# Softmax weights of six heads turned by VectorE's 32x32 blocks and placed by a trip through DRAM, where identity matmuls turned them

## The chip, the cores and the metric

The kernel runs on one core of a Trainium2 chip. The metric is device time of the whole program in microseconds (us): before the change the median of three runs is 1448.64 us (1448.3 to 1448.99). A profiled execution is read beside it. In the text TensorE is PE in the profile (PEld are its weight loads), VectorE is DVE, ScalarE is ACT, GpSimd is POOL, and SyncE is SP, which here only issues DMAs (SPq).

## The reference

A decoder trunk of two layers over 512 tokens of width 1024, in float32. Layer 0 mixes tokens by dilated sliding-window attention in three groups of eight heads, layer 1 by a gated recurrence; each layer ends in a gated feed-forward part with a short convolution, and RMS norms stand before and after every part. Only the attention matters here:

```python
WINDOWS = (128, 512, 2048); DILATIONS = (1, 4, 16); HEADS_PER_GROUP = 8; HEAD_DIM = 128
logits = einsum('bxhnqd,bxhnkd->bxhnqk', qs, kk) * scale + bias        # masked: causal band
mx = max(logits); p = exp(logits - mx); s = sum(p)
o = einsum('bxhnqk,bxhnkd->bxhnqd', p, vv) / s;  lse = mx + log(s)
...
alpha = softmax(stack(lses), axis=0)                                   # over the three groups
o = sum(alpha[..., None] * stack(outs), axis=0) @ w_o
```

For one of the eight output heads, group 0 attends within the last 128 tokens ("local"). Groups 1 and 2 attend to tokens of the same residue modulo 4 and 16 ("strided"). The kernel takes both strided groups over the four residues r of the token number modulo 4: for each r there are 128 queries and 128 keys, and the mask for residue modulo 16 lies in the bias.

## The kernel before

Nearly all time goes to matrix products of weights with activations. Each float32 operand is split into a high part `whi`, copied by ACT (line 246), and a remainder `wlo`, subtracted by DVE (line 255), and three TensorE passes make one product (`mm3`, line 423; `product`, line 611). Weight blocks of one megabyte come in on SP's queue (`raw`, line 329); some are added up from two sources by accumulating DMAs that POOL issues (`sum`, line 301). A load is issued once an earlier block has been split, so SP mostly waits for DVE's remainders.

The program is written in the order in which every engine takes its instructions; nothing reorders it. Beside the stream of products run "sides": Python generators that are advanced at each tick, that is, after each tile of 24 products. `yield n` lets n ticks pass. A strided head (`strided`, line 1289) is such a side. Per head it goes through these steps, for the two groups gi = 0, 1:

- scores: per residue one matmul q.k into PSUM (line 1310, tile S), then DVE adds the bias table `toe` and takes the row maximum (line 1314, recorded at its helper, line 1231), leaving L, 128 queries by 4 residues x 128 keys;
- ACT takes the exponential of each residue's columns with its sum (line 1299);
- DVE multiplies both L by the reciprocal of the common denominator (line 1346), and prepares the factor c0 of the local head;
- TensorE transposes each residue's 128x128 block against the identity (line 1359, tile PT), since the next product needs keys on partitions; ACT copies the result from PSUM (line 1361). A small matmul (line 1364, tile c) turns c0 the same way;
- TensorE multiplies with the values vp (line 1378, tile O), adds the local head's output ow, turned by line 1382, and the head's output oT is kept for the projection.

Heads 0 to 5 run like this in pairs, heads 6 and 7 with `ahead` set: they start earlier and use a running maximum for the first group. Tiles of 128x512 come from one pool of 29 buffers (`gen`), PSUM from 8 banks. The values are written to DRAM (line 1168) and read back by residue (line 1218), and the local heads' outputs likewise (lines 1286 and 1294), all on SP.

DMAs of SP report on eight semaphores in turn, and the program makes an issue wait until the DMA eight places ahead on the same semaphore has landed.

## Time and profile before

| | us |
|---|---|
| median of three runs | 1448.64 |
| profiled execution, span | 1446.8 |
| TensorE busy in it | 1433.7 |
| DVE busy | 1021.0 |
| ACT busy | 682.9 |
| strided heads, from the first S to the last O | about 266 to 490 |

The profiled execution's span goes from its first to its last instruction. Rows of a timeline read: start, duration, engine, line, operation, out<-in by the names of the tiles without their numbers, shapes, count, and in brackets the idle time of the engine before it and what ended it. Several equal instructions that follow each other stand in one row. Rows of groups read: count, busy time, mean duration in ns, idle time before. A float32 matmul is recorded as two rows, a transpose against the identity as one.

### The profile page before, as it was taken

To read this page: it belongs to the slowest core of one execution; us is meant where nothing else is said; L and a number is where in the kernel's file an instruction comes from. 1 tells how busy PE (TensorE), PEld (TensorE's weight loads), DVE (VectorE), ACT (ScalarE), POOL (GpSimd) and SP (SyncE) were. 2 spreads that over 40 slices of the span, in tenths; PEclk is the share of its full clock that TensorE was granted. 3 is DMA by queue.
4 is the path that set the end of the run, shared out by engine and by line. 5 is a ranking of instruction groups with operands and counts; after the bars stand their busy time and mean duration, and the time that the engine had idled before them with its cause. 6 is when DMAs were issued, how large, how long until landed. Compare 5 with 4: busy or idle time off the path is not lost.

```text
span 1446.8 us, 18794 instructions
## 1 busy us (share of the span) xinstructions
PE 1433.7 (99%) x7261; PEld 1219.0 (84%) x7261; DVE 1021.0 (71%) x1786; ACT 682.9 (47%) x1145; POOL 103.9 (7%) x116
## 2 busy tenths in 40 slices
PE   8999999999999999999999999999999999999997
PEld 6888888888888898998888888988898998888886
DVE  7864353455554688887977678877879887977675
ACT  5443332344345454455545444469654455535441
POOL 1210010111000001000000020000001000000020
PEclk9999999999999999999999999999999999999999
DMA  8974645766526153655767683233144565677561
GB/s 257 255 209 134 156 123 159 207 150 198 189 81 219 59 162 110 160 156 131 197 185 172 184 249 129 89 117 106 69 133 118 157 169 122 190 189 175 175 189 58
DMA packets 163660, 227.43 MB, mean 157 GB/s; under 512 B 6280, under 2 KB 119440, under 8 KB 163570
## 3 DMA queue, kind: packets, MB, share of 16 engines
q1 hardware_dynamic: 132544, 175.36, 36.0%
q0 software_dynamic: 31024, 50.86, 19.3%
q8 instruction: 57, 0.93, 0.3%
q14 instruction: 33, 0.27, 0.1%
q10 hardware_dynamic: 2, 0.00, 0.0%
HBM read 209.39 MB, written 21.53 MB: 160 GB/s over the span
## 4 chain that ended last, share of the span: by engine, by line
PE 97%; DVE 2%; ACT 1%; DMA 0%; issue 0%; SPq 0%; DVEq 0%
PE ps L423 55%; PE vq L611 18%; PE acc L423 11%; PE vq L423 6%; PE gate L423 2%; PE tr L472 1%; PE S L1310 1%; PE S L1243 1%; PE O L1282 1%; PE O L1378 1%; DMA raw<-in_attn_w_qkv_dram 0%; PE PT L1265 0%; PE v L1138 0%; PE PT L1359 0%; DVE wlo L178 0%; DVE wlo L255 0%
## 5 line engine op out<-in xcount | busy, mean ns | idle before, releaser
L423 PE MATMUL ps<-hT,whi 128*128 128x512 f32 (+1 forms) x2528 | 726.1, 372 | 0.6 <-DVE hT L477 0.3
L423 PEld LDWEIGHTS ps<-hT,whi 128*128 128x128 f32 x2528 | 457.6, 189 | 81.8 <-ACT whi L246 1.3
L423 PE MATMUL ps<-hT,wlo 128*128 128x512 f32 (+1 forms) x1264 | 468.3, 370 | 0.0
L255 DVE TENSOR_TENSOR wlo<-raw,whi 128x1024 fp32r<-128x1024 f32 x233 | 280.1, 1217 | 11.4 <-ACT whi L246 10.7
L423 PEld LDWEIGHTS ps<-hT,wlo 128*128 128x128 f32 x1264 | 238.1, 188 | 40.9
L246 ACT ACTIVATE whi<-raw 128x1024 fp32r<-128x1024 f32 x233 | 239.9, 1051 | 48.6 <-DMA raw<-in_ffn_w_up_dram 17.7
L796 DVE SCALAR_TENSOR_TENSOR u<-ps,cols,u 128x511 f32<-128x511 f32 (+1 forms) x160 | 119.6, 748 | 92.7 <-ACT u L792 89.9
L611 PE MATMUL vq<-whi,A 128*128 128x512 f32 x448 | 142.5, 389 | 0.0
L246 ACT ACTIVATE whi<-sum 128x1024 fp32r<-128x1024 f32 x68 | 71.4, 1053 | 113.6 <-DMA sum<-in_attn_w_qkv_dram 70.6
L255 DVE TENSOR_TENSOR wlo<-sum,whi 128x1024 fp32r<-128x1024 f32 x68 | 82.1, 1219 | 29.0 <-ACT whi L246 29.0
L423 PE MATMUL acc<-whi,ahi 128*128 128x512 f32 x256 | 100.9, 394 | 0.0
L423 PE MATMUL acc<-whi,alo 128*128 128x512 f32 x256 | 99.8, 390 | 0.0
L423 PE MATMUL acc<-wlo,ahi 128*128 128x512 f32 x256 | 99.6, 389 | 0.0
L611 PEld LDWEIGHTS vq<-whi,A 128*128 128x128 f32 x448 | 84.1, 188 | 17.6
L792 ACT ACTIVATE u<-ps,cols 128x512 f32<-128x512 f32 x80 | 61.6, 770 | 74.4 <-PE ps L423 74.4
L611 PE MATMUL vq<-wlo,A 128*128 128x512 f32 x224 | 87.1, 389 | 0.0
L806 ACT ACTIVATE u<-u 128x512 f32<-128x512 f32 x48 | 30.4, 633 | 99.7 <-DVE u L796 99.7
L611 PE MATMUL vq<-whi,T 128*128 128x512 f32 x192 | 62.2, 395 | 0.0
L423 PEld LDWEIGHTS acc<-whi,alo 128*128 128x128 f32 x256 | 48.1, 188 | 10.2
L423 PEld LDWEIGHTS acc<-wlo,ahi 128*128 128x128 f32 x256 | 48.1, 188 | 9.6
L423 PEld LDWEIGHTS acc<-whi,ahi 128*128 128x128 f32 x256 | 48.1, 188 | 9.6
L1120 DVE COPY qk<-ps 128x512 f32<-128x512 f32 x24 | 16.5, 688 | 51.2 <-PE ps L423 51.1
(250 smaller groups left out, 1814.9 us busy)
## 6 DMA issues: line engine op xcount, KB each, us to landing
raw<-in_ffn_w_up_dram SPq DMA_DIRECT2D x44, 1024.0 KB
raw<-in_attn_w_qkv_dram SPq DMA_DIRECT2D x25, 1024.0 KB
raw<-in_ffn_w_down_dram SPq DMA_DIRECT2D x16, 1024.0 KB
sum<-in_ffn_w_down_dram POOLq DMA_DIRECT2D x16, 1024.0 KB, 8.9
raw<-in_attn_w_qkv_dram SPq DMA_DIRECT2D x16, 512.0 KB
sum<-in_attn_w_qkv_dram POOLq DMA_DIRECT2D x16, 512.0 KB, 8.1
sum<-in_ffn_w_down_dram SPq DMA_DIRECT2D x8, 1024.0 KB
raw<-in_lru_w_in_dram SPq DMA_DIRECT2D x8, 1024.0 KB
```

The lines of the kernel that those rows point to most:

```text
L246: nc.scalar.activation(hi, raw, AF.Copy)
L255: nc.vector.tensor_tensor(lo, raw, hi.bitcast(F32), op=ALU.subtract)
L423: mm(dst, l[a], r[b], start=start and n == 0, stop=stop and n == 2)
L472: nc.tensor.transpose(ps[:, k * P : (k + 1) * P], xs[i][:, k * P : (k + 1) * P], ident)
L611: mm(banks[u], act(a)[:, 2 * j + k, u * P : (u + 1) * P], W[b][:, k, :], start=(j, k, n) == (0, 0, 0), stop=(j, k, n) == (1, 1, 2),)
L792: nc.scalar.activation(u, ps, AF.Identity, scale=cc[:, j : j + 1], bias=cc[:, 48 + j : 49 + j])
L796: nc.vector.scalar_tensor_tensor(u[:, d:], ps[:, : S - d], wc, u[:, d:], op0=ALU.mult, op1=ALU.add)
L806: nc.scalar.activation(u, u, AF.Gelu_apprx_tanh)
L1120: nc.vector.tensor_copy(dst, src)
L1243: mm(Sp[a // 2][:, o + lo : o + 256], q[hh][:, a * P : (a + 1) * P], k[hh][:, k0 : (a + 1) * P], start=True, stop=True)
L1282: mm(po[:, a * P : (a + 1) * P], pts[a, j], vtile(v, a - 1 + j, h % 4), start=j == js[0], stop=j == 1)
L1310: mm(ps[:, c], q[hh][:, c], k[hh][:, c], start=True, stop=True)
```

## The change

For heads 0 to 5 (not `ahead`), the turn of the weights is made without TensorE:

- L is laid out differently: `strips` puts residue r's keys 32 j to 32 j + 31 at columns 128 j + 32 r, so that scores, exponentials and the multiplication go through four runs of 32 columns per residue.
- Right after each multiplication DVE transposes L in blocks of 32x32 into a new tile LT: each block is turned in its place, but blocks are not exchanged across partitions.
- One tick later LT is written to a DRAM tile `std` (256 KB, one DMA on SP), and two ticks after that it is read back into PT by four DMAs of 64 KB on SP, which put each block where it belongs: 32 partitions, four runs of 128 elements each.
- The four transposes per group on TensorE, their PSUM bank and ACT's copy are gone. Heads 6 and 7 stay as they were. The ticks between multiplication and O are as many as before (1 + 2 + 4 against 3 + 4).

```diff
+        def strips(t):
+            return t.rearrange("p (j m k) -> p j m k", j=4, m=4)
...
+        def to_dram(t, ms, name):
+            d = dp.tile([P, 512], F32, name=name)
+            nc.sync.dma_start(strips(d)[:, :, ms, :], strips(t)[:, :, ms, :])
+            return d
+
+        def from_dram(d, ms):
+
+            t = gen(s="PT")
+            t4 = strips(t)
+            for j in range(4):
+                src = d.rearrange("(i k) (j m q) -> j k i m q", k=32, j=4, m=4)[j]
+                nc.sync.dma_start(t4[32 * j : 32 * j + 32, :, ms, :], src[:, :, ms, :])
+            return t.rearrange("p (i m q) -> p m i q", i=4, m=4)
...
+            def of_residue(L, r):
+                if ahead:
+                    return L[:, r * P : (r + 1) * P]
+                return strips(L)[:, :, r, :]
...
-                        L[:, c], L[:, c], AF.Exp, bias=neg[:, r : r + 1],
+                        of_residue(L, r), of_residue(L, r), AF.Exp, bias=neg[:, r : r + 1],
...
+                    if ahead:
+                        scores(L[:, c], ps[:, c], T[:, :P], at)
+                    else:
+                        scores(of_residue(L, r), in_strips(ps[:, c]), in_strips(T[:, :P]), at)
...
+                else:
+                    L4 = strips(L)
+                    by = of.unsqueeze(1).unsqueeze(3).to_broadcast([P, 4, 4, 32])
+                    nc.vector.tensor_tensor(L4, L4, by, op=ALU.mult)
+                    LT = gen(s="LT")
+                    nc.vector.transpose(LT, L)
+                    turned.append(LT)
...
-            yield 2 if ahead else 3
-            pts = []
-            for L in Ls:
-                ps = psum("PT")
...
+            else:
+                yield 1
+                placed = [to_dram(t, all_, f"std{h}{gi}") for gi, t in enumerate(turned)]
+                yield 2
+                pts = [from_dram(d, all_) for d in placed]
...
-                    mm(po[:, c], vtile(v, r, 2 * gi + hh), pts[gi][:, c], start=gi == 0, stop=gi == 1)
+                    mm(po[:, c], vtile(v, r, 2 * gi + hh), pts[gi][:, r], start=gi == 0, stop=gi == 1)
```

In the order of instructions this moves three places. On PE, where head 0's weights were turned, between the last product of a tile ps and the next product vq; first before the change, then now:

```order
L423 MATMUL ps_2531<-hT_86,whi_2319 128x512
L423 MATMUL ps_2531<-hT_85,wlo_2320 128x512
L1359 MATMUL PT_2558<-ident,L_2284 128x128 x4
L1359 MATMUL PT_2565<-ident,L_2296 128x128 x4
L1364 MATMUL c_2572<-s_2357,back 128x16
L611 MATMUL vq_2589<-whi_2405,T_417 128x512
```

```order
L423 MATMUL ps_2547<-hT_86,whi_2319 128x512
L423 MATMUL ps_2547<-hT_85,wlo_2320 128x512
L1407 MATMUL c_2584<-s_2361,back 128x16
L611 MATMUL vq_2601<-whi_2409,T_417 128x512
L611 MATMUL vq_2601<-wlo_2410,T_417 128x512
```

The eight transposes are gone and nothing else on PE has moved; the line of the small matmul is 1407 in the new file. On DVE, at the multiplication of head 1 (L474 and L477 are its two tiles of weights, wlo484 and wlo498 the remainders of the next two blocks of sum), now:

```order
L625 TENSOR_TENSOR v493_2474<-c489_2420,vq491_2448 128x512
...
L1368 RECIPROCAL s481_2394<-s480_2393 128x4
L1380 TENSOR_TENSOR L474_2374<-L474_2374,s481_2394 128x512
L1382 STREAM_TRANSPOSE LT494_2488<-L474_2374 128x512
L1380 TENSOR_TENSOR L477_2386<-L477_2386,s481_2394 128x512
L1382 STREAM_TRANSPOSE LT495_2491<-L477_2386 128x512
L1384 TENSOR_TENSOR s482_2395<-s482_2395,s481_2394 128x4
L1386 TENSOR_TENSOR s496_2494<-s482_2395,res_129 128x16
L255 TENSOR_TENSOR wlo484_2410<-sum54_230,whi483_2409 128x1024
L255 TENSOR_TENSOR wlo498_2497<-sum54_230,whi497_2496 128x1024
```

The two STREAM_TRANSPOSE rows are new, the rest stood there in the same order; they are now ahead of the remainders. On SP, from the write of values to the second load after it, before the change and now, with the semaphores that each waits for (DMAHW0 to DMAHW7 are the eight of SP's DMAs in turn):

```order
L329 DMA raw483_2409<-in_attn_w_qkv_dram 128x8x256 [waits DVE_49]
L1168 DMA vrows2_2411<-v490_2469 128x512 [waits DMAHW3_49,DVE_49]
L1168 DMA vrows2_2411<-v491_2470 128x512 [waits DMAHW4_49,DVE_49]
L329 DMA raw503_2529<-in_attn_w_qkv_dram 128x8x256 [waits DMAHW5_49,DVE_49]
L329 DMA raw532_2648<-in_attn_w_qkv_dram 128x4x256 [waits DMAHW6_49,DMAHW2_49,DVE_49]
L329 DMA raw532_2648<-in_attn_w_qkv_dram 128x4x256 [waits DMAHW7_49]
```

```order
L1168 DMA vrows2_2415<-v493_2474 128x512 [waits DMAHW4_49,DVE_49]
L1243 DMA std00_2479<-LT466_2355 128x512 [waits DMAHW5_49]
...
L1243 DMA std11_2535<-LT495_2491 128x512 [waits DMAHW0_49,DVE_49]
L329 DMA raw507_2545<-in_attn_w_qkv_dram 128x8x256 [waits DMAHW1_49,DVE_49]
L1252 DMA PT510_2574<-std00_2479 32x4x128 [waits DMAHW5_49,DMAHW2_49,PE_49]
L1252 DMA PT510_2574<-std00_2479 32x4x128 [waits DMAHW3_49]
...
L1252 DMA PT511_2579<-std01_2481 32x4x128 [waits DMAHW1_49]
L1252 DMA PT523_2631<-std10_2533 32x4x128 [waits DMAHW2_49,PE_49]
...
L1252 DMA PT524_2636<-std11_2535 32x4x128 [waits DMAHW1_49]
L329 DMA raw532_2656<-in_attn_w_qkv_dram 128x4x256 [waits DMAHW2_49,DVE_49]
```

The four writes stand ahead of a megabyte load and the sixteen reads of heads 0 and 1 (PT510, PT511, PT523, PT524) behind it; the next load comes after all of them. For heads 2 and 3 a load and four writes of values stand between the two groups of eight reads; for heads 4 and 5 the sixteen again follow a load, with one load of ow after the first eight.

## The prediction

> **What bounds the kernel now.** I read the head of the page first, then the chain that ended last, the waits of TensorE, and the stretch in which the strided heads run.

> ```profile
> span 1446.8 us, 18794 instructions
> PE 1433.7 (99%) x7261; PEld 1219.0 (84%) x7261; DVE 1021.0 (71%) x1786; ACT 682.9 (47%) x1145; POOL 103.9 (7%) x116
> ...
> PE 97%; DVE 2%; ACT 1%; DMA 0%; issue 0%; SPq 0%; DVEq 0%
> ...
> PE tr L472 <- DVE xs L512: 2.5, 1, 2.5
> ...
> 262.00:490.00 228.00, 227.76 (x1188) 194.19 (x1187) 121.27 (x344) 94.36 (x223) 19.18 (x24) 1.00 0.56 166
> ```

> The fourth line is the chain by engine, the fifth the longest wait that TensorE has, the last a row of the view by windows, with busy time of PE, PEld, DVE, ACT and POOL, the granted clock, the DMA share and GB/s. TensorE is busy 227.76 of 228 us in the strided heads and 97% of the chain is its own work. So a matmul row taken out there shortens the run by its own length, as long as everything that TensorE needs still comes in time, while work put on DVE (121 us of 228), ACT (94) or the queues is paid only where it makes TensorE wait. That is the whole question.

> **What is removed.** The view of the tile PT from 262 to 450 us holds the six changed heads, and the timeline of PE shows one of them:

> ```profile
> L1359 PE MATMUL PT<-ident,L x48: 270/272/273, 297.5 to 446.2; 128*128 128x128 f32 x48
> L1361 ACT ACTIVATE PT<-PT x12: 583/594/610, 308.2 to 446.7; 128x512 f32<-128x512 f32 x12
> ...
> 297.24 0.39 PE L423 MATMUL ps<-hT,wlo 128*128 128x512 f32 x1
> 297.47 1.03 PE L1359 MATMUL PT<-ident,L 128*128 128x128 f32 x8
> 298.34 0.29 PE L1364 MATMUL c<-s,back 128*128 128x16 f32 x2
> ...
> 298.80 0.40 PE L611 MATMUL vq<-wlo,T 128*128 128x512 f32 x1
> ```

> The 270 ns of one row overlap with the next, so the price is taken from starts: eight transposes from 297.47 to 298.34, 0.87 us, 0.109 each. Nothing in that list is idle before them. Six heads give 6 x 0.87 = 5.2 us. The small matmul c behind them stays. On ACT 12 x 0.594 = 7.1 us of evictions go; ACT is not on the path, so I count nothing for it.

> [...]

> **What DVE gets.** Twelve block transposes of 128x512, which no row of this kernel has. Nearest rows, of DVE from 262 to 490 us (count, busy us, mean ns):

> ```profile
> L255 DVE TENSOR_TENSOR wlo<-raw,whi 128x1024 fp32r<-128x1024 f32 x34 | 40.7, 1217 | 1.8 <-ACT whi L246 1.8
> L1346 DVE TENSOR_TENSOR L<-L,s 128x512 f32<-128x512 f32 x16 | 10.3, 688 | 0.3
> ```

> Below: nothing under half of 688 ns, since the same 512 columns are read and written; above: 1217 ns, as if it read twice as much. I take 0.69, the row of the same size: 8.3 us in all, on an engine with over 100 us to spare here. The scores, exponentials and products go through 4 x 32 instead of 128 columns in a row. They move as many elements; I take no extra, and as the upper end twice the duration.

> On average DVE has room; one stretch has not. The timeline of DVE, ACT's row of the first exponential there, and DVE's row in the windows:

> ```profile
> 283.23 0.29 DVE L1231 CUSTOM_DVE_ANT_0 L<-S,toe 128x128 f32<-128x128 f32 x1 [7.65 <-DMA toe<-skew]
> 285.82 0.39 ACT L1299 ACTIVATE L<-L,s 128x128 f32<-128x128 f32 x1
> 290.46 1.28 DVE L625 TENSOR_TENSOR v<-c,vq 128x512 f32<-128x512 f32 x2 [3.66 <-ACT c L1179]
> 292.47 1.29 DVE L1346 TENSOR_TENSOR L<-L,s 128x512 f32<-128x512 f32 x2
> 293.96 2.35 DVE L255 TENSOR_TENSOR wlo<-sum,whi 128x1024 fp32r<-128x1024 f32 x2
> ...
> 290.00:301.00 11.00, 10.09 (x19) 1.00 0.45 118
> ```

> Head 1's products stand at 292.47, right ahead of the weight remainder (wlo) that TensorE reads at 298.80. The first of the pair ends at 293.96 + 1.22 = 295.18, a margin of 3.62 us. With head 0's transposes gone TensorE is there 0.87 earlier, and two new block transposes of head 1 delay DVE by 1.38: 1.37 us are left. At 1.217 each 0.32 is left. Head 0's own two go into the 7.65 us in which DVE waited for toe. Only if scores and exponentials also double (8 x 0.29 on DVE, then 8 x 0.39 on ACT, both ahead of 290.46: 5.4 us) does it miss, by 5.1.

> The second tight place hangs on the first, because the accumulating loads of sum wait for wlo (first row, of the waits):

> ```profile
> POOL sum L301 <- DVE wlo L255: 217.6, 11, 44.6
> ...
> 307.22 1.06 ACT L246 ACTIVATE whi<-sum 128x1024 fp32r<-128x1024 f32 x1 [13.46 <-DMA sum<-in_attn_w_qkv_dram]
> 308.32 1.23 DVE L255 TENSOR_TENSOR wlo<-sum,whi 128x1024 fp32r<-128x1024 f32 x1 [7.52 <-ACT whi L246]
> 316.26 0.39 PE L611 MATMUL vq<-wlo,T 128*128 128x512 f32 x1
> ...
> 299.00:310.00 11.00, 11.00 (x55) 9.20 (x54) 2.95 (x6) 2.78 (x4) 0.33 (x1) 1.00 0.91 190
> ```

> The remainder is done at 309.55, its reader comes at 316.26: 6.71. TensorE comes 1.74 earlier (two heads), sum starts 1.38 later: 3.59 left. The DMA engines are 0.91 busy there at 190 GB/s, and the new reads come on top: head 0's 0.52 MB, 2.8 us by that rate, leave 0.8; all of both heads' 1.05 MB, 5.5 us, would be 1.9 late. I take no wait here and keep 1.9 as an upper end.

> **What the queues get.** Each changed head adds 2 writes of 256 KB and 8 reads of 64 KB to SP's queue: 12 writes, 48 reads, 6.3 MB, 28 GB/s more over these 228 us, where 166 run. The writes need not be early; the reads must have landed when TensorE reaches O (PE rows), and they are issued behind a load (SPq rows, some with two to four in one):

> ```profile
> 299.21 30.78 SPq L329 DMA_DIRECT2D raw<-in_attn_w_qkv_dram  x4
> 315.98 14.01 SPq L329 DMA_DIRECT2D raw<-in_attn_w_qkv_dram  x3
> 331.99 2.13 SPq L1218 DMA_DIRECT2D vp<-vrows  x4
> 367.88 9.12 SPq L329 DMA_DIRECT2D raw<-in_attn_w_qkv_dram  x2
> 381.25 0.92 SPq L1168 DMA_DIRECT2D vrows<-c  x2
> 425.07 11.12 SPq L329 DMA_DIRECT2D raw<-in_attn_w_o_dram  x2
> ...
> 321.48 1.95 PE L1378 MATMUL O<-PT,vp 128*128 128x128 f32 x16
> 329.19 1.95 PE L1378 MATMUL O<-PT,vp 128*128 128x128 f32 x16
> 404.89 1.95 PE L1378 MATMUL O<-PT,vp 128*128 128x128 f32 x16
> 463.11 1.95 PE L1378 MATMUL O<-PT,vp 128*128 128x128 f32 x16
> 468.11 1.95 PE L1378 MATMUL O<-PT,vp 128*128 128x128 f32 x16
> ...
> sum<-in_ffn_w_down_dram POOLq DMA_DIRECT2D x16, 1024.0 KB, 8.9
> ...
> DMA to landing us min/median/max: 2.1/2.2/15.6
> ```

> The last row is that of toe<-skew, 13 DMAs of 64 KB, the same size as the new reads. Four vp loads take 2.13 us to issue, 0.53 each. By the order of SP, sixteen reads stand behind the load at 299.21 (now 300.6, since it waits for DVE), and a read waits for the landing of the one eight places ahead; the eighth waits for that load, 8.9 us for a megabyte, 309.5. It lands at about 312.2; O of head 0 is due at 321.48 - 1.74 = 319.7, margin 7.5. Eight more issues end at 313.8, landed at 316; O of head 1 is due at 327.4, margin 11. The load queued behind them went out at 315.98, so SP is free again before it. Head 3's reads stand behind the writes at 381.25 and the load before those (out by 367.88 + 9.12 = 377.0, landed by 385.9): 392 against 404.89 - 3.5 = 401.4. Head 4's stand behind the load at 425.07 + 11.12 = 436.2: landed by 447.8 against 463.11 - 5.2 = 457.9. So no term here.

> **Sum.** 1446.8 - 5.2 = 1441.6 us for the profiled execution. The median of the runs, 1448.64, lies 1.8 above that execution; the same distance gives **1443.4 us**, 0.36% faster.

> **The rivals.**

> B, DVE or the sum loads are late. The margins of 0.32 to 1.37 and of 0.8 above are what speaks for it; that only one head pair has them speaks against it, since the other heads' transposes fall where DVE has idle time. Price 0 to 5.1 us once (a stall at the first place widens the margin of the second); with durations half way between my values and the upper ends (0.95 each, forms half longer) the miss is 2 x 0.95 + 2.7 - 2.75 = 1.9, and the time 1445.3; the full upper end gives 1448.5.

> C, the reads come late; this is the one that ends slower. If a read of 512-byte runs took what toe's slowest took, 15.6 us, the two groups of eight would need 4.3 + 31.2 us: head 1's would land at 336.1, 8.7 late, head 5's at 436.2 + 35.5 = 471.7 against 462.9, 8.8 late, head 3's at 385.9 + 4.3 + 15.6 = 405.8, 4.4 late: 22 - 5.2 = 17 us slower, 1465. It begins to stall at (327.4 - 304.9)/2 = 11 us a read and eats the gain at about 13. Against it: the median of 2.2, and that the 15.6 fell in the stretch before 283.23 in which the DMA engines were full (the DMA share is the last but one number):

> ```profile
> 270.00:278.00 8.00, 8.00 (x45) 6.90 (x45) 3.49 (x11) 4.72 (x19) 0.41 (x1) 1.00 1.15 262
> ```

> [...]

> D, the gain is swallowed behind. In the stretch from 470 to 478 DVE is nearly full and TensorE waits for it:

> ```profile
> 470.00:478.00 8.00, 8.00 (x47) 6.61 (x45) 7.65 (x21) 3.64 (x6) 0.00 (x0) 1.00 0.31 96
> 478.36 0.40 PE L1364 MATMUL c<-s,back 128*128 128x16 f32 x2 [0.24 <-DVE s L1366]
> ```

> If what fills DVE there came from loads and not from TensorE's own products, arriving 5.2 us early would only lengthen that wait, and the time would be 1446 to 1448.6. Against it: its work is evictions and remainders that follow TensorE. That the change does not remove what it says is excluded by the order of PE.

> **Chances and range.** Forecast 0.75, B 0.14, C 0.06, D 0.05. A measurement of this kernel tells about 0.2% (2.9 us) from none, so faster means under 1445.7: the forecast and half of B, 0.82; within 0.2% the other half and D, 0.12; slower is C, 0.06. The range goes from 1442.4, one microsecond below the forecast (the runs before spread by 0.7), up into B and D to 1447.0; above lie C and the ends of B and D, about 0.1.

> **What would show it.** PT rows on PE 16 where there were 64; PE busy time about 5 us less and its idle time within 1 us of before. STREAM_TRANSPOSE rows near 0.69 us; over 1.3 means B. A wait of PE at vq L611 near 298 or 315 is B, a wait of O for PT's DMA is C, a longer wait of c near 475 is D. The prediction is wrong if PE is idle more than 2 us longer than before, or if the transposes' place costs anything but 0.87 us a head.

## The result and the profile after

| | before | after |
|---|---|---|
| median of six runs each, us | 1448.80 (1448.30 to 1449.29) | 1443.75 (1442.76 to 1445.63) |
| profiled execution, span, us | 1446.8 | 1441.0 |
| TensorE busy, us | 1433.7 | 1428.5 |
| DVE busy, us | 1021.0 | 1029.0 |

The ratio is 0.9967, with a 95% interval from 0.9956 to 0.9978: the medians are 5.05 us apart, against a forecast of 5.2 (the interval reaches from 3.2 to 6.4 us). The head of the page after, and its row of the strided heads in the view by windows (columns as in the prediction):

```profile
span 1441.0 us, 18823 instructions
PE 1428.5 (99%) x7213; PEld 1212.9 (84%) x7213; DVE 1029.0 (71%) x1798; ACT 676.7 (47%) x1133; POOL 103.8 (7%) x116
...
262.00:490.00 228.00, 227.75 (x1163) 193.54 (x1162) 130.74 (x361) 90.39 (x217) 19.12 (x24) 1.00 0.66 193
```

TensorE has 48 rows less and 5.2 us less busy time, and is as full as before in the strided heads (227.75 of 228 us, 227.76 before). DVE got 9.5 us there (121.27 to 130.74), 8.5 of them the twelve block transposes, and traffic rose from 166 to 193 GB/s. The tile PT from 262 to 485 us, and DVE's two groups that the change added or reshaped:

```profile
L1252 SPq DMA_DIRECT2D PT<-std x48: 302/430/1085, 299.1 to 446.9; - x48
L1397 PE MATMUL PT<-ident,L x16: 271/272/301, 467.0 to 471.8; 128*128 128x128 f32 x16
...
L1382 DVE STREAM_TRANSPOSE LT<-L 128x512 f32<-128x512 f32 x12 | 8.5, 712 | 0.4
L1231 DVE CUSTOM_DVE_ANT_0 L<-S,toe 128x128 f32<-128x128 f32 x64 | 14.4, 286 | 14.4 <-PE S L1334 9.4 <-DMA toe<-skew 5.0
```

Sixteen transposes are left (heads 6 and 7) where there were 64. A block transpose takes 0.712 us, and a score row with four runs of 32 columns 0.286, as one with 128 in a row did (0.286 before). The timelines of TensorE, DVE, ACT and SP show the two tight places of the prediction and the reads:

```profile
293.41 2.35 DVE L255 TENSOR_TENSOR wlo<-sum,whi 128x1024 fp32r<-128x1024 f32 x2
297.13 0.39 PE L611 MATMUL vq<-wlo,T 128*128 128x512 f32 x1
...
306.67 2.02 ACT L246 ACTIVATE whi<-sum 128x1024 fp32r<-128x1024 f32 x2 [14.89 <-DMA sum<-in_attn_w_qkv_dram]
307.77 2.36 DVE L255 TENSOR_TENSOR wlo<-sum,whi 128x1024 fp32r<-128x1024 f32 x2 [7.52 <-ACT whi L246]
313.73 0.39 PE L611 MATMUL vq<-wlo,T 128*128 128x512 f32 x1
...
299.15 14.84 SPq L1252 DMA_DIRECT2D PT<-std  x16
318.95 1.95 PE L1421 MATMUL O<-PT,vp 128*128 128x128 f32 x16
462.03 1.95 PE L1421 MATMUL O<-PT,vp 128*128 128x128 f32 x16
```

The remainder of the first place is ready at 293.41 + 1.22 = 294.63 and used at 297.13: 2.50 us are left. At the second it is ready at 307.77 + 1.22 = 308.99 and used at 313.73: 4.74 are left. No O row has a wait in brackets. Against before they start 2.53 and 6.08 us earlier (heads 0 and 5: two and six heads' transposes are gone ahead of them), that is 1.74 and 5.22 for the transposes and 0.8 from the first microseconds of the execution, where TensorE waited 0.8 us for xs and not 2.5. Laid beside the kernel before, instruction by instruction, TensorE is 0.78 us ahead from 20 us on, gains 0.88 at each of the six places where a head's transposes stood, 5.3 in all, and is 6.09 ahead from there to the end. It gains and loses nothing that lasts anywhere else.

### The profile page after: what moved, and what is told of

Same layout as the page of the kernel before. It is cut to its first block, busy times and chain, and to the rows that moved or that the text cites. A ratio compares the mean times of both kernels' runs of the same rounds, so it can differ in the third digit from the quotient of the medians.

```text
span 1441.0 us, 18823 instructions
## 1 busy us (share of the span) xinstructions
PE 1428.5 (99%) x7213; PEld 1212.9 (84%) x7213; DVE 1029.0 (71%) x1798; ACT 676.7 (47%) x1133; POOL 103.8 (7%) x116
## 4 chain that ended last, share of the span: by engine, by line
PE 97%; DVE 1%; ACT 1%; issue 0%; DMA 0%; DVEq 0%; POOL 0%; ACTq 0%; POOLq 0%
PE ps L423 55%; PE vq L611 18%; PE acc L423 11%; PE vq L423 6%; PE gate L423 2%; PE S L1334 1%; PE tr L472 1%; PE S L1263 1%; PE O L1302 1%; PE O L1421 1%; PE PT L1285 0%; PE v L1138 0%; PE gain L1725 0%; DVE wlo L255 0%; DMA row<-in_norm_mix_pre_dram 0%
## 5 line engine op out<-in xcount | busy, mean ns | idle before, releaser
L423 PE MATMUL ps<-hT,whi 128*128 128x512 f32 (+1 forms) x2528 | 725.9, 372 | 0.6 <-DVE hT L477 0.3
L423 PEld LDWEIGHTS ps<-hT,whi 128*128 128x128 f32 x2528 | 457.5, 189 | 81.9 <-issue 1.3
L423 PE MATMUL ps<-hT,wlo 128*128 128x512 f32 (+1 forms) x1264 | 468.3, 370 | 0.0
L255 DVE TENSOR_TENSOR wlo<-raw,whi 128x1024 fp32r<-128x1024 f32 x233 | 280.3, 1218 | 13.4 <-ACT whi L246 12.8
L246 ACT ACTIVATE whi<-raw 128x1024 fp32r<-128x1024 f32 x233 | 239.7, 1051 | 72.5 <-DMA raw<-in_attn_w_qkv_dram 40.3
L423 PEld LDWEIGHTS ps<-hT,wlo 128*128 128x128 f32 x1264 | 238.1, 188 | 40.8
L611 PE MATMUL vq<-whi,A 128*128 128x512 f32 x448 | 142.4, 389 | 0.0
L246 ACT ACTIVATE whi<-sum 128x1024 fp32r<-128x1024 f32 x68 | 71.4, 1054 | 116.7 <-DMA sum<-in_attn_w_qkv_dram 72.4
L255 DVE TENSOR_TENSOR wlo<-sum,whi 128x1024 fp32r<-128x1024 f32 x68 | 82.1, 1219 | 30.9 <-ACT whi L246 30.9
L423 PE MATMUL acc<-whi,ahi 128*128 128x512 f32 x256 | 100.8, 394 | 0.0
L423 PE MATMUL acc<-whi,alo 128*128 128x512 f32 x256 | 99.7, 390 | 0.0
L423 PE MATMUL acc<-wlo,ahi 128*128 128x512 f32 x256 | 99.7, 389 | 0.0
L611 PEld LDWEIGHTS vq<-whi,A 128*128 128x128 f32 x448 | 84.1, 188 | 17.4
L611 PE MATMUL vq<-wlo,A 128*128 128x512 f32 x224 | 87.1, 389 | 0.0
L611 PE MATMUL vq<-whi,T 128*128 128x512 f32 x192 | 62.2, 395 | 0.0
L423 PEld LDWEIGHTS acc<-whi,alo 128*128 128x128 f32 x256 | 48.1, 188 | 10.2
L423 PEld LDWEIGHTS acc<-whi,ahi 128*128 128x128 f32 x256 | 48.1, 188 | 9.6
L423 PEld LDWEIGHTS acc<-wlo,ahi 128*128 128x128 f32 x256 | 48.1, 188 | 9.5
L611 PEld LDWEIGHTS vq<-wlo,A 128*128 128x128 f32 x224 | 42.0, 188 | 8.7
## 6 DMA issues: line engine op xcount, KB each, us to landing
raw<-in_ffn_w_up_dram SPq DMA_DIRECT2D x44, 1024.0 KB
raw<-in_attn_w_qkv_dram SPq DMA_DIRECT2D x25, 1024.0 KB
raw<-in_ffn_w_down_dram SPq DMA_DIRECT2D x16, 1024.0 KB
sum<-in_ffn_w_down_dram POOLq DMA_DIRECT2D x16, 1024.0 KB, 9.1
sum<-in_ffn_w_down_dram SPq DMA_DIRECT2D x8, 1024.0 KB
raw<-in_lru_w_in_dram SPq DMA_DIRECT2D x8, 1024.0 KB
```

Source lines behind the costliest of these rows:

```text
L246: nc.scalar.activation(hi, raw, AF.Copy)
L255: nc.vector.tensor_tensor(lo, raw, hi.bitcast(F32), op=ALU.subtract)
L423: mm(dst, l[a], r[b], start=start and n == 0, stop=stop and n == 2)
L611: mm(banks[u], act(a)[:, 2 * j + k, u * P : (u + 1) * P], W[b][:, k, :], start=(j, k, n) == (0, 0, 0), stop=(j, k, n) == (1, 1, 2),)
```

## The experiments

Theories: P, the gain is TensorE's 48 rows, and all that was added is covered; Q, the gain comes from ACT's copies and the freed PSUM banks; R, part of the trip through DRAM is still paid; and the prediction's rivals B (DVE) and C (reads late). Ratios are against the kernel before, run on the same chip with each; its median there was between 1448.19 and 1448.80 us, so medians of different runs compare to some 0.6 us.

| run | edit of the changed kernel | median us (range) | ratio, 95% interval |
|---|---|---|---|
| the change | none | 1443.75 (1442.76 to 1445.63) | 0.9967, 0.9956 to 0.9978 |
| e1_no_trip | no writes, no reads | 1442.97 (1442.06 to 1443.96) | 0.9965, 0.9952 to 0.9977 |
| e2_pe_back | 48 transposes back on TensorE | 1448.20 (1447.72 to 1448.93) | 1.0001, 0.9992 to 1.0010 |
| e3_late_reads | reads three ticks later | 1460.66 (1459.08 to 1462.53) | 1.0083, 1.0068 to 1.0098 |
| e4_short_runs | reads in runs of 128 bytes | 1443.69 (1442.52 to 1445.82) | 0.9971, 0.9960 to 0.9982 |
| e5_two | each block transpose twice | 1445.30 (1443.67 to 1447.58) | 0.9976, 0.9967 to 0.9985 |
| e5_three | three times | 1451.38 (1450.29 to 1453.48) | 1.0022, 1.0012 to 1.0031 |
| e5_four | four times | 1460.05 (1458.87 to 1462.01) | 1.0080, 1.0066 to 1.0094 |
| e5_five | five times | 1467.59 (1467.52 to 1467.77) | 1.0131, 1.0117 to 1.0144 |
| e5_six | six times | 1475.56 (1475.46 to 1477.81) | 1.0189, 1.0175 to 1.0203 |
| e6_local | the trip also for local heads 0 to 3 | 1475.09 (1474.74 to 1476.78) | 1.0184, 1.0170 to 1.0197 |
| e7_local01 | the trip also for local heads 0 and 1 | 1450.31 (1447.64 to 1452.94) | 1.0010, 1.0001 to 1.0019 |

### Without the trip

```diff
-                yield 1
-                placed = [to_dram(t, all_, f"std{h}{gi}") for gi, t in enumerate(turned)]
-                yield 2
-                pts = [from_dram(d, all_) for d in placed]
+                yield 3
+                pts = [t.rearrange("p (i m q) -> p m i q", i=4, m=4) for t in turned]
```

> The changed kernel without the trip through DRAM: the 12 writes and 48 reads are left out and O takes the block-transposed tile LT itself, so the blocks are in the wrong places and the output is not the reference's; DVE's transposes stay. Theory P (the gain is the 48 TensorE rows, 5.2 us, and the trip is fully covered): same time as the changed kernel, 1443.8 us within 1 us. Theory R (part of the trip is still paid, through later weight loads or sum loads): faster, 1441 to 1442.5. The runs of the changed kernel spread over 2.9 us, those of before over 1.0; if the added DMA traffic makes the spread, this kernel's runs spread by about 1 us again.

1442.97 us: the medians are 0.8 us apart and the intervals overlap, so the times alone tell little. The traces decide: from 20 us to the end each matmul that reads the same tiles in both (all but those of O) starts 0.26 to 0.30 us later than in the changed kernel, the same distance throughout, so TensorE nowhere pays for the trip. R falls. These five runs spread by 1.9 us, between the two values that were expected, and don't settle where the spread comes from. What the parts do behind TensorE's back can be read from one group, ACT's conversions of the weight loads (count, busy us, mean ns, then idle time before them), of before, of this run and of after:

```profile
L246 ACT ACTIVATE whi<-raw 128x1024 fp32r<-128x1024 f32 x233 | 239.9, 1051 | 48.6 <-DMA raw<-in_ffn_w_up_dram 17.7
```

```profile
L246 ACT ACTIVATE whi<-raw 128x1024 fp32r<-128x1024 f32 x233 | 239.8, 1051 | 59.2 <-DMA raw<-in_attn_w_qkv_dram 29.1
```

```profile
L246 ACT ACTIVATE whi<-raw 128x1024 fp32r<-128x1024 f32 x233 | 239.7, 1051 | 72.5 <-DMA raw<-in_attn_w_qkv_dram 40.3
```

ACT stands idle before them for 48.6 us before, 59.2 with the block transposes alone and 72.5 with the trip. The first step also holds the 7.1 us of copies that ACT no longer makes; the second is the trip alone, and of it 11.2 us end with a load's arrival (29.1 to 40.3). Loads do come later, and none of it reaches TensorE. That is what "covered" looks like in a profile.

### The transposes back on TensorE

```diff
+                for _ in range(2):
+                    ps = psum("PT")
+                    for r in range(4):
+                        nc.tensor.transpose(ps[:, r * P : (r + 1) * P], ident, ident)
```

> The changed kernel with eight 128x128 identity transposes per head put back on TensorE at the old place, as dead work: identity into a PSUM bank that nothing reads, no copy on ACT, nothing waits. Theory P: plus 6 x 0.87 = 5.2 us, 1449.0, back at the time before. Rival Q (what helped was the 12 ACT copies and the later buffers, not the TensorE rows): stays near 1443.8; half and half would give about 1446.4.

The head of the page of this run:

```profile
span 1446.1 us, 18920 instructions
PE 1432.8 (99%) x7261; PEld 1217.5 (84%) x7261; DVE 1029.2 (71%) x1798; ACT 677.0 (47%) x1133; POOL 103.8 (7%) x116
```

1448.20 us, a ratio of 1.0001: with 48 rows on TensorE that nobody reads, all of the gain is gone, while ACT is still without its twelve copies. These rows take PSUM banks again, so the time alone would not rule out the banks. But beside the changed kernel TensorE falls behind by 0.88 us at each of the six places, 5.3 in all, and nowhere else, and nothing waits there for a bank. P holds, Q falls.

### Later reads

The reads are issued three ticks later and O follows a tick behind them, at the same tick as before.

```diff
-                yield 2
+                yield 5
                 pts = [from_dram(d, all_) for d in placed]
...
-            yield 2 if ahead else 4
+            yield 2 if ahead else 1
```

> The changed kernel with the reads from DRAM issued three ticks later (1 + 5 + 1 in place of 1 + 2 + 4 ticks), the products O where they were. In the changed kernel's trace the last packets of the six heads' reads come 10 to 17 us before O. Theory P (the trip costs nothing only because of that margin): the reads of head 0 now stand behind the load issued at 314.6, need some 9.5 us as they did before, and end near 324 against O at 318.9: a wait of about 5 us at the first pair that shows as PE waiting for PT's DMA, 0 to 3 more at the other pairs, 1448 to 1452. If the reads needed much less time than read off, under 1446.

1460.66 us, 17 us over the changed kernel. The sign is right, the size is not: 13.9 us of waits came where 5 to 8 were expected, and more was lost than the waits. The waits of TensorE (total, times, longest), then its timeline at O of heads 0 and 5:

```profile
PE O L1421 <- DMA PT<-std: 13.9, 5, 6.7
```

```profile
325.84 0.77 PE L1421 MATMUL O<-PT,vp 128*128 128x128 f32 x2 [6.26 <-DMA PT<-std]
326.79 3.33 PE L1421 MATMUL O<-PT,vp 128*128 128x128 f32 x14 [0.18 <-DMA PT<-std]
...
479.47 0.76 PE L1421 MATMUL O<-PT,vp 128*128 128x128 f32 x2 [6.68 <-DMA PT<-std]
480.56 3.33 PE L1421 MATMUL O<-PT,vp 128*128 128x128 f32 x14 [0.33 <-DMA PT<-std]
```

Fourteen matmuls behind the wait take 3.33 us, where sixteen took 1.95. The view by windows gives the reason in its column of the granted clock (the third from the right):

```profile
325.00:325.80 0.80, 0.00 (x0) 0.00 (x0) 0.77 (x3) 0.80 (x2) 0.00 (x0) 0.50 0.36 92
...
330.50:331.00 0.50, 0.50 (x5) 0.50 (x4) 0.00 (x0) 0.50 (x1) 0.00 (x0) 0.50 0.00 0
331.50:332.00 0.50, 0.50 (x4) 0.41 (x3) 0.50 (x2) 0.50 (x2) 0.00 (x0) 1.00 0.00 0
```

TensorE was idle from 319.6 to 325.84. Its clock fell to 0.50 at about 324.4, 4.8 us into the wait, and came back at about 331.2, 5.4 us after work had begun again. Laid beside the changed kernel's instructions, TensorE falls behind by 9.6 us at head 0, of which 6.4 are wait, and by 9.8 at head 5, of which 7.0 are wait. The fifth wait is 0.45 us. So these two waits cost about 3 us more than their own length. It also ends the argument on C: a read that lands late does make TensorE wait at O, as C said, and dearer than C priced it.

### Short runs

The tile is written as LT stands, and the reads gather 128-byte runs where they gathered 512; the weights come to places that are not the reference's.

```diff
-                src = d.rearrange("(i k) (j m q) -> j k i m q", k=32, j=4, m=4)[j]
-                nc.sync.dma_start(t4[32 * j : 32 * j + 32, :, ms, :], src[:, :, ms, :])
+                src = bass.AP(tensor=d.tensor, offset=d.offset + 32 * j, ap=[[512, 32], [2080, 16], [1, 32]])
+                nc.sync.dma_start(t[32 * j : 32 * j + 32, :].rearrange("p (a q) -> p a q", a=16), src)
```

> The changed kernel with each of the 48 reads taking the same 64 KB into the same partitions in 512 runs of 32 elements (128 bytes) in place of 128 runs of 128 elements (512 bytes); the source addresses are others, so the output is not the reference's. Theory P: four times as many pieces lengthen the reads, but 10 us of margin cover it if a read stays under about 11 us: 1443.8 within 1.5 us. Rival C's mechanism (the length of the runs sets the time of a trip, and short ones are many times slower): a read over 11 us, O waits for PT, 1450 to 1470.

SP's row of the reads of heads 0 and 1, and TensorE's of O of head 0:

```profile
298.38 19.44 SPq L1252 DMA_DIRECT2D PT<-std  x16
...
318.66 1.95 PE L1421 MATMUL O<-PT,vp 128*128 128x128 f32 x16
```

The sixteen issues take 19.44 us where they took 14.84, 1.3 times as long and not many times, and O does not wait: 1443.69 us. From 20 us on TensorE keeps the same distance from the changed kernel within 0.08 us. Runs of 128 bytes in place of 512 cost this kernel nothing (1443.69 against 1443.75 us) while the margin holds.

### DVE's room, by dose

Each block transpose is issued n times into the same tile; every step adds 12 x 0.712 = 8.5 us to DVE.

```diff
-                    nc.vector.transpose(LT, L)
+                    for _ in range(n):
+                        nc.vector.transpose(LT, L)
```

> Each of the twelve block transposes of the changed kernel is issued four times into the same tile (same output), to price DVE's first tight place. By the changed kernel's trace a transpose takes 0.71 us, DVE waits 5.0 us for toe behind head 0's, and the remainder wlo ahead of 297 us has a margin of 2.50 us. Head 0's extra 6 x 0.71 = 4.3 us go into the 5.0 us; head 1's extra 4.3 us pass the margin by 1.8. Theory W (a wait costs its own length): TensorE waits 1.8 us at vq, 1445.5 us. Theory K (an idle TensorE also loses its clock for about 5 us, as it did in the run with late reads once it had been idle for 4.8 us): the same here, since 1.8 us is too short. If the forecast's margins are worth nothing, 0 or over 4 us.

> Each block transpose issued five times. Head 0's extra 8 x 0.71 = 5.7 us exceed the 5.0 by 0.7, head 1's 5.7 pass the margin: 0.7 + 5.7 - 2.5 = 3.9 us of wait at vq. W: 1447.7 us and a granted clock of 1.00 behind the wait. K: the same as W if 3.9 us is too short for the clock to fall, 1450 to 1451 with a granted clock of 0.50 for about 5 us behind the wait if it is not.

> Each block transpose issued six times. Head 0's extra 10 x 0.71 = 7.1 us exceed the 5.0 by 2.1, head 1's 7.1 pass the margin: 2.1 + 7.1 - 2.5 = 6.7 us of wait at vq. W: 1450.5 us. K: the granted clock falls to 0.50 for about 5 us and some 3 us come on top, 1453 to 1454. DVE's other extra work, 60 x 0.71 = 43 us in all, costs nothing under both.

These three came out 14 to 25 us above what was expected. So two smaller doses followed:

> Each block transpose issued twice (same output): 1.43 us each, above the upper bound of 1.217 that the prediction set. If its margins hold: head 1's extra 1.43 us leave 1.1 of the 2.50 us at vq, nothing waits, the changed kernel's 1443.8 us. If DVE has no room at all, each pair is late by 1.4 us and the time is 1446 or more.

> Each block transpose issued three times. Head 1's extra 2.9 us pass the 2.50 by 0.4; with toe landing up to 1.7 us later, as with four, by 2.1: one wait of 0.4 to 2.1 us at vq, none elsewhere (with four the waits behind it came to 1.1 at head 2's and 3's c, 1.3 at S, 2.2 at acc; each head has 1.4 us less to carry here), no fall of the clock: 1444.2 to 1446 us. If the series goes straight from one to four (16.3 us for three steps): 1454.6.

From one to six the time goes 1443.75, 1445.30, 1451.38, 1460.05, 1467.59, 1475.56: the first 8.5 us on DVE cost 1.6 (the intervals of one and two overlap; the wait below shows that it is real), the next 6.1, and from then on each costs 7.5 to 8.7, nearly its own length. TensorE's first wait at vq, in its timeline with two, three, four and six, shows the forecast's place. With two there is no row with a wait there, and with the others:

```profile
297.81 0.50 PE L611 MATMUL vq<-wlo,T 128*128 128x512 f32 x1 [0.43 <-DVE wlo L255]
```

```profile
301.51 0.80 PE L611 MATMUL vq<-wlo,T 128*128 128x512 f32 x1 [3.53 <-DVE wlo L255]
```

```profile
305.24 0.79 PE L611 MATMUL vq<-wlo,T 128*128 128x512 f32 x1 [7.23 <-DVE wlo L255]
```

0.43 against an expected 0.4 to 2.1 with three, 3.53 against 1.8 with four, 4.2 against 3.9 with five, 7.23 against 6.7 with six: the margin of 2.50 at vq is real, and with four the missing 1.7 us are toe's, for which DVE waited twice there, 1.0 and 1.1 us. What the expectations had not seen is that vq is not the only place, nor the first. With five and six TensorE waits longer at c, for DVE's factors s, than at vq (8.0 and 11.4 us in two waits each). With two, the only new wait behind the first 20 us is yet another, and its cause can be followed through three engines (TensorE, ACT and SP in the run with two, then SP in the changed kernel):

```profile
473.33 1.23 PE L1398 MATMUL PT<-ident,L 128*128 128x128 f32 x8 [1.22 <-DVE L L1376]
...
457.48 1.06 ACT L246 ACTIVATE whi<-raw 128x1024 fp32r<-128x1024 f32 x1 [10.30 <-DMA raw<-in_attn_w_o_dram]
...
424.99 10.44 SPq L1243 DMA_DIRECT2D std<-LT  x4
...
451.88 0.40 SPq L329 DMA_DIRECT2D raw<-in_attn_w_o_dram  x1
```

```profile
422.64 8.95 SPq L1243 DMA_DIRECT2D std<-LT  x4
...
447.74 0.40 SPq L329 DMA_DIRECT2D raw<-in_attn_w_o_dram  x1
```

DVE turns heads 4 and 5 later; the writes of LT on SP wait for it; a weight load, the sixteen reads of these heads and another load stand behind the writes, and that other load goes out some 4 us later (451.88 against 447.74); ACT, whose conversions stand in the program's order, waits 10.3 us for it, and the exponentials of heads 6 and 7 stand behind that conversion; DVE multiplies late, and TensorE waits 1.22 us for that. With three, c (0.9 us) and acc (1.0) join, and PT has 3.4 in two waits; with vq's 0.4 these are 5.7 of the 7.8 us between the spans (1448.8 and 1441.0). Beside the changed kernel TensorE falls behind at these five places alone, by 7.7 us: each wait costs 0.2 to 0.6 us more than the idle time in its bracket, with the clock at 1.00.

The clock fell in these runs too. The longest wait of the run with three, and one near the end of the run with four:

```profile
473.14 1.23 PE L1398 MATMUL PT<-ident,L 128*128 128x128 f32 x8 [2.19 <-DVE L L1376]
```

```profile
477.33 0.50 PE L423 MATMUL acc<-whi,ahi 128*128 128x512 f32 x1 [2.15 <-ACT ahi L177]
```

Behind the first the granted clock stayed at 1.00, behind the second it fell. The windows of the run with four, behind its 3.53 us and behind its 2.15 us:

```profile
301.00:302.00 1.00, 0.49 (x1) 0.49 (x2) 1.00 (x2) 0.00 (x0) 0.00 (x0) 0.50 0.61 236
...
306.00:307.00 1.00, 1.00 (x4) 0.81 (x3) 0.93 (x4) 0.00 (x0) 0.00 (x0) 0.50 1.18 183
...
478.00:480.00 2.00, 2.00 (x6) 1.59 (x6) 0.60 (x2) 1.99 (x3) 0.00 (x0) 0.59 1.03 410
```

It was at 0.50 from about 300.9, 2.9 us into the first wait, to 307.7, and TensorE fell behind by 6.7 us there, 3.1 more than the wait. Behind the 2.15 us it was at 0.50 for 3.4 us, and TensorE fell behind by 4.2, 2.1 more than the wait. Theory K, that an idle TensorE also loses its clock, holds in kind; the length of 4 us and more that it had in mind does not, since 3.53 and once 2.15 us sufficed. W (a wait costs its own length) falls for these two waits. What parts the 2.15 us from the 2.19 is not shown.

### The same edit in another place

The edit for local heads 0 to 3; the run after it has `h < 2` in the first line.

```diff
+            if h < 4:
+                placed = []
+                for c in range(2):
+                    o = P if c == 0 else 0
+                    LT = gen(s="LT")
+                    nc.vector.transpose(LT[:, o:], L[c][:, o:])
+                    d = dp.tile([P, 512], F32, name=f"loc{h}{c}")
+                    nc.sync.dma_start(d[:, o:], LT[:, o:])
+                    placed.append(d)
+                yield 1
...
+                        for b in range(b0, 4):
+                            nc.sync.dma_start(dst[:, b], src[:, b])
```

> The same edit in another place: the weights of local heads 0 to 3 are turned by eight block transposes on DVE (0.71 us each) at the step of their 28 identity transposes, written to DRAM, and read back into the same tiles a step later in 28 reads of 16 KB a head. The rule from the runs so far (TensorE's rows count by their starts, all else is covered): 28 x 0.109 = 3.1 us less than the changed kernel, 1440.7 us. The rival: the reads hold up the weight loads behind them on SP's queue (56 issues of 0.4 us for two heads, 22 us against margins of 15 to 23 us there) and TensorE waits, or O waits for PT: 1444 us or more.

1475.09 us. TensorE's waits, its first wait in its timeline, and SP's row of head 2's reads:

```profile
PE O L1324 <- DMA PT<-loc: 27.4, 4, 11.6
```

```profile
143.03 1.62 PE L1324 MATMUL O<-v,PT 128*128 128x128 f32 x6 [11.59 <-DMA PT<-loc]
```

```profile
136.73 13.13 SPq L1298 DMA_DIRECT2D PT<-loc  x28
```

TensorE came 0.79 us earlier at each of the four removed groups of seven (0.76 by the count), and lost far more at O of heads 2 and 3. The waits were there from the start of head 2's O: it was due at 143.03 - 11.59 = 131.4, and its 28 reads were issued from 136.7 to 149.9. (One tick more per head also moves head 2's O ahead of head 0's, since its step now falls behind the arrival of the values. So the 31 us are not the price of the reads alone.) Heads 0 and 1 have the time, so they were tried alone:

> The trip for local heads 0 and 1 alone. In the run with four local heads TensorE came 0.79 us earlier at each of the four removed groups of seven, and the waits of O for PT were those of heads 2 and 3, which have 11 to 12 us between the turn and O, while heads 0 and 1 have 43 or more. So 2 x 0.79 = 1.6 us less than the changed kernel: 1442.2 us, the fastest. The rival: the 56 reads on SP's queue (32 us of issue) hold the weight loads up and TensorE waits for weights: 1444 or more.

1450.31 us: 6.6 us slower than the changed kernel and as slow as the kernel before (1.0010). The rival's time came true, by another way than the one written down. SP's timeline, then ACT's and DVE's, then TensorE's:

```profile
91.68 17.35 SPq L1298 DMA_DIRECT2D PT<-loc  x28
...
111.09 14.76 SPq L1298 DMA_DIRECT2D PT<-loc  x28
125.95 10.64 SPq L329 DMA_DIRECT2D raw<-in_attn_w_qkv_dram  x5
```

```profile
131.55 1.06 ACT L246 ACTIVATE whi<-raw 128x1024 fp32r<-128x1024 f32 x1 [13.78 <-DMA raw<-in_attn_w_qkv_dram]
```

```profile
132.64 1.23 DVE L255 TENSOR_TENSOR wlo<-raw,whi 128x1024 fp32r<-128x1024 f32 x1 [11.33 <-ACT whi L246]
134.38 0.68 DVE L1312 COPY PT<-PT 128x512 f32<-128x512 f32 x1
```

```profile
135.12 1.16 PE L1324 MATMUL O<-v,PT 128*128 128x128 f32 x8 [2.68 <-DVE PT L1312]
138.13 1.62 PE L1324 MATMUL O<-c,PT 128*128 128x128 f32 x6 [1.85 <-DVE c L625]
```

The weights themselves would still have come in time: no wait of TensorE for a weight tile appears. But DVE waits 11.33 us for the high part of one, and head 3's copy out of PSUM, which TensorE needs at once, is queued behind that. Two waits of 2.68 and 1.85 us follow, and the clock at 0.50 from about 136 to 143.

## Why the prediction held, point by point

**Bound by TensorE, and what is removed.** Held, to the row: 0.87 us a head was forecast, 0.88 is measured in both directions, and putting the rows back takes the whole gain away.

**What DVE gets.** The block transpose was taken as 0.69 us and measured 0.712; the strided forms cost nothing, as taken (a multiplication 0.671 against 0.688, an exponential 0.388 both times). The first tight place was to keep 1.37 us and keeps 2.50: head 1's scores began at 281.25 and not at 283.23, because toe came 2.0 us earlier; 0.8 of that is the shift of the whole execution, the other 1.2 were not foreseen. The second was to keep 0.8 and keeps 4.74. There the term was mis-sized: the sum loads were to start 1.38 us later and to be slowed by 2.8 us of reads, but the remainder was ready at 308.99, 0.56 earlier than before (0.2 later, if the shift of 0.8 is taken off), at 233 GB/s (190 before, in the same stretch from 299 to 310):

```profile
299.00:310.00 11.00, 11.00 (x51) 9.14 (x50) 3.41 (x6) 3.33 (x4) 0.00 (x0) 1.00 1.10 233
```

So the reads came largely on top of the traffic, not in its place (the DMA share went from 0.91 to 1.10, so 0.91 was not full), and rival B had less behind it than the prediction gave it.

**"An engine with over 100 us to spare."** True as an average and of no use: the doses show that about 9 us more, spread over six heads, were nearly free and the next 9 were not. The prediction looked for DVE's limits at vq and along the sum loads, not along the weight loads on SP. The place that gave way first lies nearly 40 us behind the transposes that caused it (435 to 473 us), by way of SP and ACT.

**What the queues get.** The sixteen reads of heads 0 and 1 were to be issued by 313.8 and were by 299.15 + 14.84 = 313.99; the eighth, held until the load ahead had landed, went out at 308.6 (309.5 forecast). That the ends agree so well is in part luck: the load went out 1.9 us earlier than taken and landed 9.9 us after its issue, not 8.9. No O waited. Rival C is a real mechanism: brought about on purpose it costs 17 us, which is more than its waits.

**Rival D** had no part: the change's 5.3 us are in the end of the run in full. But its stretch, around 473 us, is the one that stalls first when DVE gets more work.

**The sum.** 1441.6 was forecast for the profiled execution and 1441.0 came. The change is worth the 5.3 us above, which alone would give 1441.5; the rest of the 5.8 between the spans comes from the beginning, which differs from execution to execution. By medians it is 1443.4 against 1443.75. What the prediction did not foresee is the spread: 2.9 us in six runs, where before had 1.0. The profiled executions differ in their first 20 us, in how long TensorE waits for xs and whether its clock falls there (0.91 in before's, 1.00 in after's):

```profile
0.00:20.00 20.00, 15.74 (x50) 10.45 (x50) 11.65 (x27) 12.00 (x28) 3.96 (x12) 0.91 0.84 284
```

```profile
0.00:20.00 20.00, 16.57 (x52) 9.70 (x52) 12.25 (x29) 12.65 (x29) 3.95 (x12) 1.00 0.88 298
```

That this makes the spread of the runs without a profile is argued, not shown, and the mean granted clock does not order the changed kernel's six (0.998 at 1442.76 us, 0.999 at 1444.55, 0.997 at 1445.63). The change need not be its cause: 27 runs of the kernel before in the last comparison spread by 2.8 us as well.

## What to carry to other kernels

Where one engine is full in a stretch, a row taken from it is worth the distance of its starts there (0.11 us here, where its own duration is 0.27), and the price of the replacement is whether each of its parts has a margin; find the margin from the trace, then take the edit to the next place only after finding it there anew, since the same edit lost 7 and 31 us where they were other. An engine's spare time cannot be read from its share of the span: look at what is queued behind the new work on every in-order queue, SP's and ACT's included, and who waits for that. The waits of TensorE that were followed here cost their own length and 0.2 to 0.6 us (the run with three) or, where the clock came down, 2.1 to 3.2 us on top (the runs with late reads and with four).

## What was not expected of the hardware

So a wait of about 2.2 us cost 0.2 to 0.6 us more than its length in one run (2.19 us, with three) and 2.1 more in another (2.15 us, with four). Behind three of the longer waits (6.3 and 6.7 us with late reads, 3.5 with four transposes) the loss could be followed instruction by instruction: about 3 us each on top of the wait, with the clock at 0.50 for 6.8 us.
